# One unit of q less beside the first modulation, two half units of distance in the first GLA head, and fewer modulation steps on TensorE in the branch stage

## The chip, the cores and the metric

The kernel runs on one core of one Trainium2 chip. The metric is the device time of one launch in microseconds. The four compute engines of the core are called by the profile's names: PE (TensorE, matrix products), DVE (VectorE), ACT (ScalarE), POOL (GpSimd). SP issues most DMAs, POOL's queue issues those of the later modulation weights.

## The reference

One layer of a hybrid backbone on 384 tokens of width 2048: 128 context tokens and 256 latent tokens, held side by side as the 384 columns of every product. Cut to what matters here:

```
mod = silu(cond) @ w_ada + b_ada                  # 2048 -> 6 * 2048, for 2 conditions
sh1, sc1, ga1, sh2, sc2, ga2 = split(mod, 6)
h = rmsnorm(x) * (1 + sc1) + sh1
q, k, v, g, lr_f, lr_b, fo = split(h @ w_in)      # q, k: 4 heads x 128, v: 4 x 256
o = gla(q, k, v, decay(lr_f), decay(lr_b))        # chunked scan, both directions, 4 heads
f = real(fft2(fo))                                # per group of 256 channels
gates = sigmoid(h @ w_gate + b_gate)              # 2 * 2048
m = (g_a * (o * silu(g)) @ w_br_gla + g_b * (f @ w_br_four)) @ w_out
x = x + ga1 * rmsnorm(m)
h = rmsnorm(x) * (1 + sc2) + sh2
x = x + ga2 * rmsnorm((silu(h @ w_ffn_gate) * (h @ w_ffn_up)) @ w_ffn_down)
```

All inputs and results are fp32.

## The kernel before, in words

**Products.** Each fp32 operand is split into a high part, a cast to fp32r, and a low part, the difference. A product is three matmuls: high by high, high by low, low by high. For a weight, ACT writes the high part (`whi<-raw`, L300) and DVE the low part (`wlo<-raw`, L287); for an activation the same pair is L378 and L379. A *unit* is 128 output features for all 384 tokens: `proj` runs it as two *half units*, and `gemm` (L326, written `pmm`) issues 24 matmuls of 384 columns for each half unit.

**The first stage** (loop over `kb` from 0 to 15, 128 features of h each). For each `kb`, PE first makes the 256 numbers of shift and scale: `gemv` (L474, `pgm<-slab,spad`) multiplies the condition vector with two slabs of `w_ada1`, 1 MB each, which SP loads into five buffers. Two transposes (L595) and a few DVE instructions turn them into columns, DVE writes the modulated features, ACT and DVE split them. While that runs, PE works on the features of the `kb` before: the product of all of v (`vprod`, L491, `pv`, three groups of six matmuls), and `XU` units of q (`xprod`, L509, three matmuls each for one unit), whose weights `xraw` come in a transfer of their own. Unit 0 uses the PSUM bank `px`, unit 1 from `kb` 3 on the bank `pgm`, which the modulation uses too. DVE adds each finished piece to `xacc` (L504). The order of every engine but SP is that of the code.

**The query, key and gate stage.** The units of q and k that the first stage did not make follow as ordinary units, in the order of `qk_order`, and then 25 units of the gate product. Each half unit but the first unit's calls `side()`, which takes one step of two generators: `gla()`, the small operations of the attention heads, and `ada`, the rest of the modulation. Where `gla()` has a `yield`, the next half unit is put between. In a head, the two directions prepare `qi`, `ki`, `kc`, `ko` on DVE (L851 to L858), one step each. Then PE makes the scores `at` (L875, twelve matmuls for each direction) and `cr`, DVE masks them (L885), some steps later DVE and ACT split `ko` and `att`, and PE makes the state update `dl` and the output `po` (L788).

**The rest of the modulation.** `ada_rest` has six blocks of 1024 columns. A block has 16 `k`-steps, each on a piece of `w_ada` of 512 KB that POOL's queue loads into two buffers (`adaw`). A step runs in one of two ways, by the flag `on_pe`: on DVE as two multiply-adds of 128x1024 (L707, `adacc`), or on PE as four matmuls of 128x256 (L697, `pr<-adaw,spad`). After the steps of a block come an empty call, a call that sums the block over partitions on PE (L718) and one with its transposes (L671).

**The branch stage.** The output gate `g` of the attention and the two branch products are made in `mix_order`: 8 units "o" with a `side()` of their own, 16 pieces "b" of the Fourier branch (`four`, L1239 and L1240), and 16 units "a" of the attention branch, one `gemm` of 24 matmuls each. The first "o" units take modulation steps through `side()` (on PE from its turn 7 on, but for turn 8); the "a" units that the table `TAIL` lists take one each, on PE where it says True. After each "a" unit DVE multiplies by the gate (L1296) and adds (L1297), and one unit later the result is split into `A_hi` and `A_lo` (L379), the right operand of the product with `w_out` that follows. That product's first unit needs `A_lo` of all 16 pieces. The modulation steps that are left run beside `w_out`.

```
if i in TAIL:
    on_pe[0] = TAIL[i]
    next(ada_gen, None)
    on_pe[0] = False
```

Of the kernel before, what the change touches and what calls it, by code (L numbers as in the profile page):

```python
# [25 lines left out]
T = TC + TL  # L26
# [8 lines left out]
FC = 4  # L35
NFC = FT // FC
G = 1024
XU = 2
GF = 25
GD = 256  # L40
TAIL = {1: True, 4: False, 5: True, 8: True, 10: False, 11: True, 13: True, 14: False, 15: False}


C_TRI = 0
# [63 lines left out]
def tile_step(ctx: ExitStack, tc: tile.TileContext, a, o):  # L108
# [49 lines left out]
    srcs = [a["w_v"][k] for k in range(KT)]  # L158
    qk_order = [i for i in (4, 5, *range(XU, 4), 6, 7)]
    for i in qk_order:  # L160
# [250 lines left out]
    with ExitStack() as s:  # L411
# [11 lines left out]
        def load_w(kb):  # L423
            load()
            xraw[kb] = pb.tile([P, XU * P], F32, tag="xraw", name="xraw", bufs=2)
            SP.dma_start(xraw[kb], a["w_x"][kb])
# [39 lines left out]
        pgm = pss.tile([P, 512], F32, tag="side", name="pgm")  # L466
        pgv, pmod = pgm[:, 0:256], pgm[:, 256:512]
        px = pss.tile([P, T], F32, tag="side", name="px")
# [27 lines left out]

        xacc = [pa.tile([P, T], F32, name=f"xacc{u}") for u in range(XU)]
        lracc = pa.tile([P, T], F32, name="lracc")
# [7 lines left out]
        def xprod(u, kb, w, bank=px):  # L506
            def mm():
                for j, (x_, w_) in enumerate(passes(w)):
                    PE.matmul(bank, w_[:, u * P : (u + 1) * P], hT[x_][:, kb, :], start=j == 0, stop=j == 2)  # L509

            return mm, lambda dst=None: flush(xacc[u], kb == 0, dst, bank)
# [38 lines left out]
        prev = None  # L550
        for kb in range(KT):
            if kb and kb + 1 < KT:
                load_slab(kb + 1)
                load_w(kb + 1)
                if kb == 4:
                    load_later()

            wait = kb in (1, 2)
            if kb and not wait:
                gemv(kb)  # L560
            todo = []
            if kb > 4 and kb % 4 == 2:
                todo.append(lrprod(kb - 6))

            both = kb > 2
            if both:
                xs = [xprod(u, kb - 1, prev[1], bank) for u, bank in enumerate((px, pgm[:, 0:T]))]
            elif kb:
                todo += [xprod(u, kb - 1, prev[1]) for u in range(XU)]
            todo += [None] * (4 - len(todo))  # L570
            flushes = [t[1] if t else lambda: None for t in todo]

            def pe_x(n):
                if todo[n]:
                    todo[n][0]()

            if wait:
                vprod(kb - 1, prev[0], (0,))
            pe_x(0)
            hf = scr[:, kb % 8, :]  # L580

            xr = hf if kb else qs[0]
            DVE.tensor_mul(xr, xn(kb), rstd if kb else px)
            flushes[0]()
            if wait:
                gemv(kb)
            if kb:
                ev = pb.tile([P, 256], F32, tag="ev", name="ev")
                ACT.copy(ev, pgv)
            lag = []  # L590
            new = split_w(kb, lag)
            if kb:
                vprod(kb - 1, prev[0], (1 if wait else 0,))
            for m in range(2):
                PE.transpose(pmod[:, m * P : (m + 1) * P], ev[:, m * P : (m + 1) * P], ident)  # L595
            if kb == 0:

                for _ in range(6):
                    PE.matmul(pv[5][:, 0:P], ones, ones, start=True, stop=True)
            pe_x(1)  # L600

            pm = pb.tile([P, 2, 2], F32, tag="pm", name="pm", bufs=2)
            DVE.tensor_reduce(
                pm, pmod.rearrange("p (m q r) -> p m r q", m=2, q=4)[:, :, 0:2, :], axis=mybir.AxisListType.X, op=ALU.add,
            )
            DVE.tensor_scalar(
                mods[:, 1, kb, :], pm[:, 1, :], bsc1[:, 0, kb : kb + 1], norms[:, 0, kb : kb + 1],
                op0=ALU.add, op1=ALU.mult,
            )
            DVE.tensor_scalar_add(mods[:, 0, kb, :], pm[:, 0, :], cols[:, 0, kb : kb + 1])  # L610
            for lo, hi, c in segs:
                DVE.tensor_scalar(
                    hf[:, lo:hi], xr[:, lo:hi], mods[:, 1, kb, c : c + 1], mods[:, 0, kb, c : c + 1],
                    op0=ALU.mult, op1=ALU.add,
                )
                if kb == 0:
                    ACT.activation(
                        hT[0][:, kb, lo:hi], xr[:, lo:hi], AF.Identity,
                        bias=mods[:, 0, kb, c : c + 1], scale=mods[:, 1, kb, c : c + 1],
                    )  # L620
            flushes[1]()
            if kb:
                split_act(hT[0][:, kb, :], hT[1][:, kb, :], hf)
            else:
                ACT.copy(rstd, px)
                DVE.tensor_sub(hT[1][:, kb, :], hf, hT[0][:, kb, :].bitcast(F32))
            if kb:
                if not wait:
                    vprod(kb - 1, prev[0], (1,))
                pe_x(2)  # L630
                flushes[2]()
            if both:
                for mm, _ in xs:
                    mm()
                for _, fl in reversed(xs):
                    fl()
            for sub in lag:
                sub()
            if kb:
                vprod(kb - 1, prev[0], (2,))  # L640
                pe_x(3)
                flushes[3]()
            prev = new
# [109 lines left out]
    with ExitStack() as s:  # L753
# [25 lines left out]
        def gla():  # L779
# [10 lines left out]
            for h in range(NH):  # L790
# [38 lines left out]
                for d in range(2):  # L829


                    bT = pss.tile([P, T], F32, tag="side", name="bT")
                    for t in range(3):
                        for j, l in enumerate((lah, lal)):
                            PE.matmul(
                                bT[:, t * P : (t + 1) * P], l[:, t, d], tri[:, d * P : (d + 1) * P],
                                start=j == 0, stop=j == 1,
                            )
                    sx = pss.tile([P, 2, P], F32, tag="side", name="sx")
                    for j, l in enumerate((lah, lal)):  # L840
                        PE.matmul(
                            sx, tri[:, (2 + d) * P : (3 + d) * P], l[:, 0 : 2 + d : 1 + d, d], start=j == 0, stop=j == 1,
                        )
                    eb = pg.tile([P, T], F32, tag=f"eb{d}", name="eb")
                    ACT.activation(eb, bT, AF.Exp)
                    ki = pg.tile([P, T], F32, tag=f"ki{d}", name="ki")
                    ACT.activation(ki, bT, AF.Exp, scale=-1.0)
                    ko = pg.tile([P, 2, P], F32, tag=f"ko{d}", name="ko")
                    ACT.activation(ko, sx, AF.Exp)
                    qi = pg.tile([P, T], F32, tag=f"qi{d}", name="qi")  # L850
                    DVE.scalar_tensor_tensor(qi, eb, DK**-0.5, qT[:, h, :], op0=ALU.mult, op1=ALU.mult)  # L851
                    DVE.tensor_mul(ki, ki, kT[:, h, :])
                    DVE.tensor_mul(ko, ko, krs[:, 0 : 2 + d : 1 + d, :])

                    last = 0 if d else CH - 1
                    tot = chunks(eb)[:, :, d, last : last + 1]
                    kc = pg.tile([P, 3, CH], F32, tag=f"kc{d}", name="kc")
                    DVE.tensor_mul(kc, chunks(ki)[:, :, d, :], tot.to_broadcast([P, 3, CH]))  # L858
                    dc = pg.tile([P, 1], F32, tag=f"dc{d}", name="dc")
                    c = 5 if d else 2  # L860
                    e0, e1 = c * CH + last, (c + 1 - 2 * d) * CH + last
                    DVE.tensor_mul(dc, eb[:, e0 : e0 + 1], eb[:, e1 : e1 + 1])
                    qin.append(qi)
                    kin.append(ki)
                    kcr.append(kc)
                    kout.append(ko)
                    dec.append((tot, dc))
                    yield

                ats = []  # L870
                for d in range(2):
# [33 lines left out]
                ap = [apt[:, 0], apt[:, 1]]  # L905
                split_act(*ap, att)
                yield
                qpt = [pg.tile([P, 2, 3, P], F32R, tag=t, name="qp") for t in ("lah", "lal")]
                qp = [[q[:, d] for q in qpt] for d in range(2)]
                for d in range(2):  # L910
# [88 lines left out]
    px = fs.enter_context(tc.tile_pool(name="px", bufs=1))  # L999
# [310 lines left out]
    with ExitStack() as s:  # L1310
# [94 lines left out]
        u = pd.tile([P, 2, 3], F32, name="u12", bufs=1)  # L1405
# [355 lines left out]
        bank = {}  # L1761
# [69 lines left out]
        for kind, c, i in steps[:-4]:  # L1831
# [8 lines left out]
            if kind == "D":  # L1840
# [9 lines left out]
                h = hid_last if last_c else hid  # L1850
# [248 lines left out]
```

## Time and profile before

| | us |
|---|---|
| median of three runs | 1943.53 |
| the three runs | 1943.53, 1943.78, 1941.89 |
| the profiled execution | 1942.28 |
| its span | 1940.4 |
| PE busy | 1920.4 (99%) |
| DVE busy | 1647.8 (85%) |
| ACT busy | 916.3 (47%) |

The clock that the throttle granted TensorE was 0.998 of full speed. The time of an execution has 1.9 us that lie outside the span (1942.28 less 1940.4). A row of the timeline gives the start, the duration, the engine, the line, the operation with what it writes and reads, and a count where like instructions follow each other; a bracket at its end says how long the engine was idle before it and what ended that.

### The profile page before, as it was taken

To read this page: it belongs to the slowest core of one execution; us is meant where nothing else is said; L and a number is where in the kernel's file an instruction comes from. 1 tells how busy PE (TensorE), PEld (TensorE's weight loads), DVE (VectorE), ACT (ScalarE), POOL (GpSimd) and SP (SyncE) were. 2 spreads that over 40 slices of the span, in tenths; PEclk is the share of its full clock that TensorE was granted. 3 is DMA by queue.
4 is the path that set the end of the run, shared out by engine and by line. 5 is a ranking of instruction groups with operands and counts; after the bars stand their busy time and mean duration, and the time that the engine had idled before them with its cause. 6 is when DMAs were issued, how large, how long until landed. Compare 5 with 4: busy or idle time off the path is not lost.

```text
span 1940.4 us, 27538 instructions
## 1 busy us (share of the span) xinstructions
PE 1920.4 (99%) x10534; PEld 1690.8 (87%) x10534; DVE 1647.8 (85%) x2172; ACT 916.3 (47%) x1298; POOL 85.8 (4%) x154
## 2 busy tenths in 40 slices
PE   9999999999999999999999999999999999999997
PEld 5779999999999999999988888888888888888886
DVE  5668898889878887978789888999998999888885
ACT  4235455545456554456455444444444444444444
POOL 0001111100000000104000000000000000000001
PEclk9999999999999999999999999999999999999999
DMA  9977766766757885755264636363636272625243
GB/s 390 387 260 248 240 234 227 248 231 194 225 185 246 302 302 181 245 193 198 83 195 131 200 103 194 121 211 98 216 104 213 91 222 93 201 76 185 87 173 110
DMA packets 200615, 380.52 MB, mean 196 GB/s; under 512 B 14196, under 2 KB 126932, under 8 KB 196132
## 3 DMA queue, kind: packets, MB, share of 16 engines
q1 hardware_dynamic: 181252, 320.84, 48.9%
q0 software_dynamic: 13952, 50.39, 8.5%
q10 hardware_dynamic: 5280, 7.55, 1.1%
q8 instruction: 82, 1.34, 0.3%
q14 instruction: 49, 0.40, 0.1%
HBM read 361.94 MB, written 16.78 MB: 195 GB/s over the span
## 4 chain that ended last, share of the span: by engine, by line
PE 93%; DVE 3%; DMA 2%; issue 1%; ACT 1%; SPq 0%; DVEq 0%; ACTq 0%
PE pgu L338 30%; PE pmm L326 30%; PE pdn L338 18%; PE pv L491 3%; PE pgm L474 1%; PE pf L1239 1%; PE pfo L1039 1%; DVE adacc L707 1%; PE pmm L1516 1%; PE ptr L1808 1%; PE pf L1240 1%; PE pfo L1040 1%; DMA xraw<-in_w_x 1%; PE po L788 1%; PE px L509 0%
## 5 line engine op out<-in xcount | busy, mean ns | idle before, releaser
L326 PE MATMUL pmm<-A_hi,whi 128*128 128x384 f32 x1072 | 361.7, 337 | 0.0
L326 PE MATMUL pmm<-A_hi,wlo 128*128 128x384 f32 x1072 | 358.8, 335 | 0.0
L326 PE MATMUL pmm<-A_lo,whi 128*128 128x384 f32 x1072 | 358.6, 335 | 0.0
L1663 ACT CAST whi<-u 128x1024 fp32r<-128x1024 f32 x200 | 210.6, 1053 | 281.5 <-DVE u L1647 86.5
L1663 ACT CAST whi<-raw 128x1024 fp32r<-128x1024 f32 x175 | 184.2, 1052 | 200.8 <-PE pgu L338 63.8
L1674 DVE TENSOR_TENSOR wlo<-u,whi 128x1024 fp32r<-128x1024 f32 x200 | 244.1, 1220 | 32.0 <-ACT whi L1663 18.3
L338 PE MATMUL pgu<-whi,A_hi 128*128 128x512 f32 x640 | 250.0, 391 | 0.0
L338 PE MATMUL pgu<-whi,A_lo 128*128 128x512 f32 x640 | 249.3, 389 | 0.0
L1674 DVE TENSOR_TENSOR wlo<-raw,whi 128x1024 fp32r<-128x1024 f32 x175 | 213.4, 1220 | 34.6 <-ACT whi L1663 25.6
L287 DVE TENSOR_TENSOR wlo<-raw,whi 128x1024 fp32r<-128x1024 f32 x163 | 198.2, 1220 | 24.1 <-ACT whi L300 23.7
L300 ACT CAST whi<-raw 128x1024 fp32r<-128x1024 f32 x149 | 156.0, 1051 | 117.6 <-PE pmm L326 50.0
L326 PEld LDWEIGHTS pmm<-A_hi,whi 128*128 128x128 f32 x1072 | 201.2, 188 | 3.3 <-issue 2.5
L326 PEld LDWEIGHTS pmm<-A_lo,whi 128*128 128x128 f32 x1072 | 201.4, 188 | 0.2
L326 PEld LDWEIGHTS pmm<-A_hi,wlo 128*128 128x128 f32 x1072 | 201.2, 188 | 0.3 <-DVE wlo L287 0.2
L707 DVE SCALAR_TENSOR_TENSOR adacc<-adaw,spad,adacc 128x1024 f32<-128x1024 f32 x160 | 198.1, 1279 | 3.5 <-DMA adaw<-in_w_ada 3.2
L338 PE MATMUL pdn<-whi,hid_hi 128*128 128x512 f32 x480 | 186.9, 389 | 0.0
L338 PE MATMUL pdn<-whi,hid_lo 128*128 128x512 f32 x480 | 186.8, 389 | 0.0
L338 PE MATMUL pgu<-wlo,A_hi 128*128 128x512 f32 x640 | 184.2, 389 | 0.0
L338 PEld LDWEIGHTS pgu<-whi,A_hi 128*128 128x128 f32 x640 | 120.2, 188 | 26.1 <-issue 0.8
L338 PEld LDWEIGHTS pgu<-wlo,A_hi 128*128 128x128 f32 x640 | 120.1, 188 | 25.4
L338 PEld LDWEIGHTS pgu<-whi,A_lo 128*128 128x128 f32 x640 | 120.1, 188 | 25.0
L338 PE MATMUL pgu<-whi,S 128*128 128x512 f32 x480 | 131.1, 395 | 0.0
(405 smaller groups left out, 3042.7 us busy)
## 6 DMA issues: line engine op xcount, KB each, us to landing
adaw<-in_w_ada POOLq DMA_DIRECT2D x96, 512.0 KB, 4.0
raw<-in_w_d SPq DMA_DIRECT2D x88, 512.0 KB, 3.7
slab<-in_w_ada SPq DMA_DIRECT2D x32, 1024.0 KB, 10.2
raw<-in_w_gate SPq DMA_DIRECT2D x64, 512.0 KB, 4.4
raw<-in_w_g SPq DMA_DIRECT2D x48, 512.0 KB, 3.4
raw<-in_w_u SPq DMA_DIRECT2D x48, 512.0 KB, 3.5
raw<-in_w_in SPq DMA_DIRECT2D x44, 512.0 KB, 4.3
u<-in_w_u SPq DMA_DIRECT2D x40, 512.0 KB, 4.6
```

The source lines that it names most:

```text
L287: eng.tensor_sub(lo, raw, hi.bitcast(F32))
L300: ACT.copy(hi, raw)
L326: PE.matmul(dst, w[wi][:, k * n + n0 : k * n + n0 + P], x[xi][:, k0 + k, :], start=first and k == 0 and j == 0, stop=last and k == kts - 1 ...
L338: PE.matmul(dst, stat[x_][m], mov(w[w_], m), start=first and w_ == m == x_ == 0, stop=last and w_ == m == 1,)
L474: PE.matmul(pgv[q : q + 32, :], spad[:, k, :], slab[k // (KT // 2)][:, k % (KT // 2), :], start=k < 4, stop=k >= KT - 4,)
L491: PE.matmul(pv[2 * t + g], hT[x_][:, kb, t * P : (t + 1) * P], w_[:, g * 512 : (g + 1) * 512], start=kb == 0 and j == 0, stop=kb == KT - 1 ...
L707: DVE.scalar_tensor_tensor(acc[:, c, :], w, spad[:, k, c : c + 1], acc[:, c, :], op0=ALU.mult, op1=ALU.add,)
L788: PE.matmul(dst, w[wi], x[xi], start=first and j == 0, stop=last and j == 2)
L1039: PE.matmul(p, w_of[0][:, i, k, g, :], x[:, :, lo:hi], start=kt == 0, stop=False)
L1040: PE.matmul(p[:, 0], w_of[1][:, i, k, g, :], x[:, 0, lo:hi], start=False, stop=kt == KT - 1)
L1663: ACT.copy(hi, src)
L1674: DVE.tensor_sub(lo, src, hi.bitcast(F32))
```

## The change

It does three things. `XU` goes from 2 to 1: the first stage makes q's unit 0 alone, `xraw` is 64 KB and not 128 KB for each `kb`, and unit 1 of q stands as an ordinary unit in `qk_order` after k's units 0 and 1. In head 0 of `gla()` two more `yield`s are put in, one ahead of the scores and one ahead of the state update, so that each of these comes one half unit later after what it reads. In `TAIL` the five places with True are gone or False: 1 and 5 drop out, 8, 11 and 13 run on DVE; the steps of 4, 10, 14 and 15 stay on DVE.

```diff
-XU = 2
+XU = 1
...
-TAIL = {1: True, 4: False, 5: True, 8: True, 10: False, 11: True, 13: True, 14: False, 15: False}
+TAIL = {4: False, 8: False, 10: False, 11: False, 13: False, 14: False, 15: False}
...
             if both:
-                xs = [xprod(u, kb - 1, prev[1], bank) for u, bank in enumerate((px, pgm[:, 0:T]))]
+                xs = [xprod(u, kb - 1, prev[1], bank) for u, bank in enumerate((px, pgm[:, 0:T])[:XU])]
...
                     dec.append((tot, dc))
                     yield
+                if h == 0:
+                    yield
 
                 ats = []
...
                 split_act(*ap, att)
                 yield
+                if h == 0:
+                    yield
                 qpt = [pg.tile([P, 2, 3, P], F32R, tag=t, name="qp") for t in ("lah", "lal")]
```

Counted over the whole program, PE has 48 fewer `xprod` matmuls and 48 more of `pmm`, and 20 fewer of `pr<-adaw`, which are five modulation steps; DVE has ten more L707, which are the same five steps. The number of calls of `ada` up to the start of `w_out` is 87 before and now: the two half units of q's unit 1 take two steps in the query stage, and two places of `TAIL` are gone.

On PE in the first stage, in a `kb` of which both units stood, the difference reads (`px` and `pgm` are the two banks, `pv` is v's):

```order
 L509 MATMUL px<-A_hi,wlo 128x384
 L509 MATMUL px<-A_lo,whi 128x384
-L509 MATMUL pgm<-A_hi,whi 128x384
-L509 MATMUL pgm<-A_hi,wlo 128x384
-L509 MATMUL pgm<-A_lo,whi 128x384
 L491 MATMUL pv<-whi,A_lo 128x512 x6
 L474 MATMUL pgm<-slab,spad 32x256 x16
```

The three matmuls of unit 1 are gone; v's last group and the next `gemv` follow unit 0 directly.

On DVE in head 0, from the second direction's preparation of `ki` to the masking of the scores, before:

```order
L852 TENSOR_TENSOR ki<-ki,qk 128x384
L853 TENSOR_TENSOR ko<-ko,krs 128x256
L858 TENSOR_TENSOR kc<-ki,eb 128x192
L862 TENSOR_TENSOR dc<-eb 128x1
L707 SCALAR_TENSOR_TENSOR adacc<-adaw,spad,adacc 128x1024 x2
L287 TENSOR_TENSOR wlo<-raw,whi 128x1024
L885 COPY_PREDICATED att<-mask,at 64x3x64 x2
```

At the same place now (the first new `yield` shifts the line numbers behind it by two):

```order
L852 TENSOR_TENSOR ki<-ki,qk 128x384
L853 TENSOR_TENSOR ko<-ko,krs 128x256
L858 TENSOR_TENSOR kc<-ki,eb 128x192
L862 TENSOR_TENSOR dc<-eb 128x1
L707 SCALAR_TENSOR_TENSOR adacc<-adaw,spad,adacc 128x1024 x2
L287 TENSOR_TENSOR wlo<-raw,whi 128x1024
L707 SCALAR_TENSOR_TENSOR adacc<-adaw,spad,adacc 128x1024 x2
L287 TENSOR_TENSOR wlo<-raw,whi 128x1024
L887 COPY_PREDICATED att<-mask,at 64x3x64 x2
```

One modulation step and one weight split more stand between the preparation and the masking.

On DVE in the branch stage, at the "a" units 10 and 11, the difference reads (L1296 and L1297 are now L1300 and L1301):

```order
 L243 TENSOR_TENSOR ws<-raw 128x512
 L244 TENSOR_TENSOR ws<-raw 128x512
-L1296 TENSOR_TENSOR gate<-gate,pmm 128x384
-L1297 TENSOR_TENSOR yb<-yb,gate 128x384
+L1300 TENSOR_TENSOR gate<-gate,pmm 128x384
+L1301 TENSOR_TENSOR yb<-yb,gate 128x384
 L379 TENSOR_TENSOR A_lo<-yb,A_hi 128x384
+L707 SCALAR_TENSOR_TENSOR adacc<-adaw,spad,adacc 128x1024 x2
 L287 TENSOR_TENSOR wlo<-ws,whi 128x1024
 L287 TENSOR_TENSOR wlo<-raw,whi 128x1024
```

The modulation step of unit 11 now stands on DVE, ahead of two weight splits.

## The prediction

> **What bounds the kernel now.** I read the page first: the busy times, and the chain of work that ended last.
>
> ```profile
> span 1940.4 us, 27538 instructions
> PE 1920.4 (99%) x10534; PEld 1690.8 (87%) x10534; DVE 1647.8 (85%) x2172; ACT 916.3 (47%) x1298; POOL 85.8 (4%) x154
> PE 93%; DVE 3%; DMA 2%; issue 1%; ACT 1%; SPq 0%; DVEq 0%; ACTq 0%
> ```
>
> PE is idle for 20 us of the span. So a matmul taken off PE is worth its time, where nothing else makes PE wait at that place; and a matmul put on costs its time. All three parts of the change have to be priced as PE time first, and then each place has to be looked at for what comes late instead. I looked at them in the order of the program: the chain of waits in the first stage, its transfers, the timeline of PE and DVE in the first attention head, and the same two in the branch stage.
>
> **The change part by part: the first stage.** The chain there, and one row of the weight loads' timeline:
>
> ```profile
> 40.53 1.39 PE pv L491 x6
> 41.92 0.54 PE px L509 x3
> 42.45 0.53 PE pgm L509 x3
> 42.98 1.39 PE pv L491 x6
> 44.37 1.86 PE pgm L474 x32
> 60.13 0.61 PEld L474 LDWEIGHTS pgm<-slab,spad 128*32 128x32 f32 x16 [0.25 <-DMA slab<-in_w_ada]
> 128.80 1.86 PE pgm L474 x32
> ```
>
> Unit 1's three matmuls are the 0.53 us on `pgm`. There are 16 such groups, one for each `kb`, so PE loses 16 x 0.53 = 8.5 us of work. That is the upper bound of this part's gain. Not all of it can count: at 60.13 the second half of `kb` 6's `gemv` started the moment its slab had landed (PE's loader had been idle 0.25 us for it), so up to there the stage goes no faster than its transfers.
>
> ```profile
> slab<-in_w_ada SPq DMA_DIRECT2D x10, 1024.0 KB, 11.1
> raw<-in_w_v SPq DMA_DIRECT2D x5, 512.0 KB, 8.1
> xraw<-in_w_x SPq DMA_DIRECT2D x5, 128.0 KB, 8.0
> 20.00:50.00 30.00, 29.51 (x229) 20.32 (x228) 18.55 (x44) 9.81 (x19) 0.00 (x0) 1.00 1.02 414
> 60.00:85.00 25.00, 25.00 (x209) 17.70 (x202) 15.62 (x37) 7.04 (x14) 0.00 (x0) 1.00 1.02 414
> 85.00:125.00 40.00, 40.00 (x314) 28.80 (x313) 24.57 (x57) 11.80 (x22) 0.00 (x0) 1.00 0.97 359
> ```
>
> The last number of a windows row is GB/s. A `kb` moves two slabs, one `raw` and one `xraw`: 2.75 MB before, 2.69 MB now (half of `xraw`, 65.5 KB, is gone). Up to `kb` 6 that is about six halves, 0.39 MB, at 414 GB/s 0.95 us sooner. From there on the `gemv` of `kb` 7 to 15 have nine groups fewer ahead of them, and two more groups lie behind the last `gemv`: 11 x 0.53 = 5.8 us, if the slabs keep up. Together the gain is 6.8 us.
>
> Do the slabs keep up? The last two were issued right after PE had read a slab for the last time:
>
> ```profile
> L474 PE MATMUL pgm<-slab,spad x2: 379/379/379, 114.6 to 114.6; 128*32 128x256 f32 x2
> L419 SPq DMA_DIRECT2D slab<-in_w_ada x2: 382/382/382, 114.9 to 115.4; - x2
> DMA to landing us min/median/max: 10.6/10.6/10.6
> ```
>
> The last landed at 115.4 + 10.6 = 126.0, and the second half of the last `gemv` needed it at about 128.80 + 0.93 = 129.7. So there was 3.7 us of slack at the end of the stage against nearly none at `kb` 6: the transfers had gained on PE. Now PE gains 9 x 0.53 = 4.8 us on that stretch, and the transfers' issue, which waits for PE to free a buffer, comes earlier with it, and 9 x 65.5 KB less are to be moved (0.59 MB, 1.4 us at 414 GB/s). A slack of 3.7 + 1.4 = 5.1 covers 4.8, so I take 6.8. The bounds are 8.5, as if nothing waited, and 4.3, from the first rival.
>
> **Unit 1 of q as a unit of its own.** It costs 48 matmuls of `pmm`.
>
> ```profile
> 673.21 4.21 PE pmm L326 x24
> 677.42 0.57 PE pr L697 x8
> 677.99 8.55 PE pmm L326 x48
> 720.90 29.33 PE pmm L326 x168
> ```
>
> In a long run one takes 29.33/168 = 0.1746 us, so 48 take 8.4 us. Its weights add two transfers of 512 KB and two splits, in a stage that has one of each for every half unit already. A half unit gives DVE 4.2 us for one split (1.21) and one modulation step (2.47, both below), so I charge nothing more. This eats the first stage's gain and more: −6.8 + 8.4 = +1.6.
>
> **The first attention head.** PE's timeline at head 0, with DVE's rows beside it, the pair of score groups of the next head (from the chain), and what the state update waits for:
>
> ```profile
> 191.34 0.57 PE L875 MATMUL at<-qi,ki 128*64 128x64 f32 x12
> 193.46 0.57 PE L875 MATMUL at<-qi,ki 128*64 128x64 f32 x12 [1.55 <-DVE ki L852]
> 260.96 0.85 PE at L875 x24
> 191.16 1.21 DVE L287 TENSOR_TENSOR wlo<-raw,whi 128x1024 fp32r<-128x1024 f32 x1
> 192.30 0.54 DVE L851 SCALAR_TENSOR_TENSOR qi<-eb,qk 128x384 f32<-128x384 f32 x1
> 192.77 0.54 DVE L852 TENSOR_TENSOR ki<-ki,qk 128x384 f32<-128x384 f32 x1
> 211.38 0.72 PE dl L788 x6
> 210.49 0.75 DVE L379 TENSOR_TENSOR part<-ko,part 128x256 fp32r<-128x256 f32 x2
> ```
>
> The second direction's scores start 193.46 − 191.34 = 2.12 us after the first's, where a group takes 0.85/2 = 0.43: PE waits 1.7 us for `ki`, which DVE ends at 193.31. The first new `yield` puts a half unit of 4.2 us ahead of the scores, and DVE makes `ki` as early as before (the order of its rows up to there is the same). So the scores are wanted at about 195.5, `ki` is there 2.2 us sooner, and the 1.7 us go. That also takes away the delay behind which `dl` found its operands: it started at 211.38, and DVE's `part` of `ko` had ended at 211.24, 0.14 before. Without the second `yield`, PE coming 1.7 us earlier there would wait for most of it again; with it there are again 4.2 us between. Gain 1.7, its bounds 0 and 1.7.
>
> **Five modulation steps from PE to DVE.** On PE a step costs its own 0.57 us and a little around it: the rows from 673.21 to 686.54 take 4.21 + 0.57 + 8.55 = 13.33 us for 72 matmuls, which at 0.1746 would take 12.57. So 0.76 each, and 3.8 us for five.
>
> On DVE each costs two L707. Three of the five stand in the "a" units that stay (8, 11, 13); DVE's timeline there:
>
> ```profile
> 706.88 2.47 DVE L707 SCALAR_TENSOR_TENSOR adacc<-adaw,spad,adacc 128x1024 f32<-128x1024 f32 x2
> 709.27 0.69 DVE L243 TENSOR_TENSOR ws<-raw 128x512 f32<-128x512 f32 x1
> 698.12 0.56 DVE L1296 TENSOR_TENSOR gate<-gate,pmm 128x384 f32<-128x384 f32 x1 [1.00 <-PE pmm L326]
> 702.28 0.55 DVE L1296 TENSOR_TENSOR gate<-gate,pmm 128x384 f32<-128x384 f32 x1 [1.41 <-PE pmm L326]
> 717.99 0.55 DVE L1296 TENSOR_TENSOR gate<-gate,pmm 128x384 f32<-128x384 f32 x1 [0.97 <-PE pmm L326]
> 725.30 0.55 DVE L1296 TENSOR_TENSOR gate<-gate,pmm 128x384 f32<-128x384 f32 x1 [1.50 <-PE pmm L326]
> 736.47 1.23 DVE L379 TENSOR_TENSOR A_lo<-yb,A_hi 128x384 fp32r<-128x384 f32 x2
> ```
>
> A step takes DVE 709.27 − 706.88 = 2.39 us, so three add 7.2. In the brackets DVE stood idle for PE for 1.00 + 1.41 + 0.97 + 1.50 = 4.9 us, which the added work fills. The steps of units 1 and 5 are gone from PE before this stretch, so DVE, which waits for PE there, enters it 2 x 0.76 = 1.5 us earlier. Left over is 7.2 − 4.9 − 1.5 = 0.8: the last `A_lo`, done at 736.47 + 1.23 = 737.70, is done at 738.5. PE wants it in the first unit of `w_out`, at the 119th of the 168 matmuls from 720.90 (72 of units 13 to 15, then 15 pieces of three, then the one by the low part): 720.90 + 118 x 0.1746 = 741.5, a slack of 3.8. But PE is now 3.8 us earlier, and wants it at 737.7. It waits 0.8 us. The bounds are 0 and 1.5, if the 1.5 us are not passed on. The other two added DVE steps take the places of `side()` turns in the "o" units where PE had them; a "o" half unit gives DVE the same 4.2 us, and I charge nothing.
>
> **The sum.** −6.8 + 8.4 − 1.7 − 3.8 + 0.8 = −3.1 us. The profiled execution took 1942.28 (1.9 us around its span), and with the three runs the mean of four is 1942.9. I take 1942.6 as the base, between the two: 1942.6 − 3.1 = 1939.5. By the profiled execution alone it would be 1939.2, by the median of 1943.53 it would be 1940.4.
>
> **The rivals.** *The transfers hold the first stage.* The third windows row moved only 359 GB/s. If that is all that the queue gives from `kb` 6 on, a `kb` takes 2.69 MB/359 GB/s = 7.48 us, and from 60.13 less 0.95 the slab of `kb` 15 comes at 59.2 + 9 x 7.48 = 126.5 in place of the need at 129.7: 3.2 us gained there and 1.1 behind it, 4.3 in all. The sum is then −0.6, the time 1942.0. Against it: in that stretch PE took (128.80 − 60.13)/9 = 7.63 us for a `kb`, and 2.75 MB in 7.63 us is 361 GB/s, which is what PE asked for; and the rows before it have 414. [...]
>
> *The first stage gains all of it.* If the wait at 60.13 comes from a slab that fewer bytes and an earlier free buffer bring earlier, all 16 groups count and the branch stage loses nothing: −8.5 + 8.4 − 1.7 − 3.8 = −5.6, so 1937.0. For it: the wait at 60.13 is only 0.25 us. Against it: slabs were already landing at the full 414 GB/s there.
>
> *VectorE becomes the bound of the branch stage.* The idle in the brackets is time in which DVE waited for PE; if something that DVE itself feeds (a weight's low part) comes late for PE at units 8 to 13, PE stops, and the brackets fill no longer. Then the 7.2 us of the three steps come through whole instead of 0.8: the sum is −3.1 + 6.4 = +3.3, the time 1945.9, slower than before. It decides as soon as DVE's delay passes the slack that the weight splits have, which by the last `A_lo` is 3.8 us before and nothing now. Against it: DVE stood idle for PE at four units' gates in the rows above.
>
> *The wait of the first head stays.* If the scores or `dl` wait as long at their new place, 1.7 us are lost again: 1941.2. Against it stands 2.2 us of slack.
>
> **How the numbers follow.** The forecast has 0.55, the transfers 0.15, the full gain 0.14, VectorE 0.10, the wait that stays 0.06. About 0.2% (3.9 us) is what a measurement of this kernel can tell from no change, so faster begins below 1939.6 and slower above 1947.4. The forecast lies on the lower of these bounds, its own range being 1937.5 (the lower base of 1942.28 and all 8.5 us of the first stage) to 1941.1 (the median as the base and a wait of 1.5 for `A_lo`); I count 0.28 of it as faster and 0.27 as the same. The full gain adds 0.14 to faster: 0.42. The transfers, the wait that stays and half of VectorE's case are within: 0.27 + 0.15 + 0.06 + 0.05 = 0.53. The other half of VectorE's case, with a second wait behind the first, is slower: 0.05. The range goes from 1936.0, the full gain less half the 1.9 us by which the three runs differ, to 1944.5, which takes in the transfers and the part of VectorE's case in which half of the 6.4 us comes through, and leaves out the rest.
>
> **What would show it right or wrong.** In the profile after: the chain of the first stage should have no `pgm L509`, and the last `gemv` should start near 128.80 − 0.95 − 4.8 = 123.1; a bracket with `slab` at `kb` 10 to 15 would be the first rival. The second `at` group should follow the first by 0.4 us, and `dl` should have no bracket. The rows `pr L697` among the "a" units should be gone, with PE's "a" units following each other by 4.2 us and one wait under 1.5 us for `A_lo` some 50 matmuls into `w_out`. A bracket with `wlo` or `A_lo` of several microseconds would prove the VectorE case. A time above 1944.5 would mean that a wait came in which I did not see; one below 1936.0 that PE's idle, not its work, was what the change took away.

## The result, and the profile after

| | before | after |
|---|---|---|
| median | 1942.61 (22 runs) | 1939.58 (22 runs) |
| lowest to highest | 1941.39 to 1944.13 | 1938.76 to 1940.83 |
| the profiled execution, its span | 1942.28, 1940.4 | 1939.26, 1937.5 |

The ratio is 0.9985, with a 95% interval of 0.9979 to 0.999. The forecast was 1939.5, 3.1 us less than its base of 1942.6; measured are 3.0 us less. The page of the changed kernel, the same three lines as of before:

```profile
span 1937.5 us, 27470 instructions
PE 1916.2 (99%) x10494; PEld 1689.0 (87%) x10494; DVE 1650.8 (85%) x2168; ACT 915.3 (47%) x1301; POOL 85.8 (4%) x154
PE 92%; DMA 3%; DVE 3%; ACT 1%; issue 0%; SPq 0%; DVEq 0%; ACTq 0%
```

PE has 4.2 us less work (the 40 instructions fewer are the 20 matmuls of the five modulation steps, each of which the profile shows as two), and the span is 2.9 us shorter. PE's idle time grew by 1.3 us (1937.5 − 1916.2 against 1940.4 − 1920.4). To see where, take the two programs at places that both have, first of the kernel before and then of the changed one: the first matmuls of the first k unit (a row with two times gives the start of the first and of the last matmul that it counts), the second head's scores (before, they stand in the prediction, at 260.96), the first modulation step on PE in the o units, and the block's sum beside `w_out`:

```profile
L326 PE MATMUL pmm<-A_hi,whi x2: 338/342/346, 142.3 to 142.8; 128*128 128x384 f32 x2
...
L697 PE MATMUL pr<-adaw,spad x8: 379/391/403, 590.6 to 590.8; 128*32 128x256 f32 x8
...
750.23 1.00 PE pr L718 x16
```

```profile
L326 PE MATMUL pmm<-A_hi,whi x14: 333/334/346, 135.8 to 142.6; 128*128 128x384 f32 x14
...
260.88 0.85 PE at L877 x24
...
L697 PE MATMUL pr<-adaw,spad x8: 379/391/403, 590.5 to 590.7; 128*32 128x256 f32 x8
...
747.57 1.00 PE pr L718 x16
```

The first stage ends 6.5 us sooner (142.3 to 135.8). At the next head's scores the lead is 0.1, and 0.1 at 590: the unit of q, less the head's wait, has taken it. The lead comes back between 590 and 750: 2.7 us (750.23 to 747.57). So nearly all of the net gain is made in the branch stage, as the sum had it (−0.1 up to there, −3.0 in it).

The details, first of the first stage: the loader's row at `kb` 6, the chain at the end of the stage, then two windows whose last number is GB/s.

```profile
59.46 0.59 PEld L474 LDWEIGHTS pgm<-slab,spad 128*32 128x32 f32 x16 [1.39 <-DMA slab<-in_w_ada]
121.48 0.54 PE px L509 x3
122.02 1.40 PE pv L491 x6
123.41 1.86 PE pgm L474 x32
60.00:85.00 25.00, 25.00 (x199) 17.57 (x192) 13.75 (x36) 7.71 (x15) 0.00 (x0) 1.00 1.02 413
85.00:120.00 35.00, 35.00 (x288) 24.25 (x287) 20.67 (x49) 10.15 (x20) 0.00 (x0) 1.00 0.98 380
```

`pgm L509` is gone. The wait at `kb` 6 is longer, 1.39 us in place of 0.25, and the second half of that `gemv` starts 0.67 sooner (60.13 to 59.46), not 0.95. The last `gemv` starts at 123.41, against 123.1 expected and 128.80 before. The last windows row has 380 GB/s where it had 359: the queue gave more when PE asked for more, and no `gemv` after `kb` 6 waits for its slab. That closes the first rival, whose rate of 359 was PE's demand.

Then the head: DVE's `ki`, PE's chain.

```profile
186.64 0.55 DVE L852 TENSOR_TENSOR ki<-ki,qk 128x384 f32<-128x384 f32 x1
136.01 8.35 PE pmm L326 x48
189.11 0.85 PE at L877 x24
211.32 0.72 PE dl L788 x6
```

Both score groups run in one piece, 0.85 us, and `ki` (ended at 187.19) was there 2.3 us before its group at 189.5; 2.2 were expected. A unit of 48 matmuls takes 8.35.

Then the branch stage: two `pf` matmuls of the chain as they run without a wait, the places where PE waits, the last two `A_lo` (pieces 14 and 15, in one row), and the chain from the first wait for them to the block's sum:

```profile
599.98 0.20 PE pf L1243
600.18 0.09 PE pf L1244
612.24 0.34 PE L1243 MATMUL pf<-edT,whi 128*128 128x388 f32 x1
612.86 0.36 PE L1244 MATMUL pf<-edT,wlo 128*128 128x194 f32 x1 [0.28 <-DVE wlo L287]
613.05 0.36 PE L1243 MATMUL pf<-edT,whi 128*128 128x388 f32 x1
...
737.33 1.22 DVE L379 TENSOR_TENSOR A_lo<-yb,A_hi 128x384 fp32r<-128x384 f32 x2
737.30 0.34 PE L326 MATMUL pmm<-A_hi,whi 128*128 128x384 f32 x1
737.94 0.44 PE L326 MATMUL pmm<-A_lo,whi 128*128 128x384 f32 x1 [0.30 <-DVE A_lo L379]
738.22 0.34 PE L326 MATMUL pmm<-A_hi,wlo 128*128 128x384 f32 x1
...
738.61 0.44 PE L326 MATMUL pmm<-A_lo,whi 128*128 128x384 f32 x1
738.89 0.34 PE L326 MATMUL pmm<-A_hi,wlo 128*128 128x384 f32 x1
...
737.94 9.63 PE pmm L326 x53
```

The block's sum comes behind 96 matmuls of `w_out` (in the prediction's row of 168, 72 belong to the units), and 53 of them run from 737.94 on. So the matmul that waited there is the 44th of `w_out`, in the prediction's count the 116th, which reads the `A_lo` of piece 14; the 119th, with that of piece 15, follows at 738.61, when the row of `A_lo` has ended (738.55; the prediction had 738.5). From 737.30 to 738.89 PE started five matmuls in 1.59 us in place of 0.87, so the two together cost 0.7; 0.8 was expected, at the 119th alone. The stall on a weight's low part at 612.86 was not: 0.81 us from 612.24 to 613.05, where such a pair takes 0.20 + 0.09, so 0.5.

### The profile page after: what moved, and what is told of

It reads as the page before. It is cut to its first block, busy times and chain, and to the rows that moved or that the text cites. A ratio compares the mean times of both kernels' runs of the same rounds, so it can differ in the third digit from the quotient of the medians.

```text
span 1937.5 us, 27470 instructions
## 1 busy us (share of the span) xinstructions
PE 1916.2 (99%) x10494; PEld 1689.0 (87%) x10494; DVE 1650.8 (85%) x2168; ACT 915.3 (47%) x1301; POOL 85.8 (4%) x154
## 4 chain that ended last, share of the span: by engine, by line
PE 92%; DMA 3%; DVE 3%; ACT 1%; issue 0%; SPq 0%; DVEq 0%; ACTq 0%
PE pgu L338 31%; PE pmm L326 31%; PE pdn L338 18%; PE pv L491 3%; DMA slab<-in_w_ada 2%; PE pfo L1043 1%; PE pf L1243 1%; PE pgm L474 1%; PE pmm L1520 1%; PE ptr L1812 1%; PE pfo L1044 1%; PE pf L1244 1%; PE po L788 1%; DVE wlo L287 0%; DMA raw<-in_w_br_gla 0%
## 5 line engine op out<-in xcount | busy, mean ns | idle before, releaser
L326 PE MATMUL pmm<-A_hi,whi 128*128 128x384 f32 x1088 | 366.9, 337 | 0.0
L326 PE MATMUL pmm<-A_lo,whi 128*128 128x384 f32 x1088 | 364.1, 335 | 0.3 <-DVE A_lo L379 0.3
L326 PE MATMUL pmm<-A_hi,wlo 128*128 128x384 f32 x1088 | 364.2, 335 | 0.0
L707 DVE SCALAR_TENSOR_TENSOR adacc<-adaw,spad,adacc 128x1024 f32<-128x1024 f32 x170 | 210.4, 1279 | 3.3 <-DMA adaw<-in_w_ada 3.1
```

The source lines that it names most:

```text
L326: PE.matmul(dst, w[wi][:, k * n + n0 : k * n + n0 + P], x[xi][:, k0 + k, :], start=first and k == 0 and j == 0, stop=last and k == kts - 1 ...
L707: DVE.scalar_tensor_tensor(acc[:, c, :], w, spad[:, k, c : c + 1], acc[:, c, :], op0=ALU.mult, op1=ALU.add,)
```

## The experiments

Each kernel was timed beside the kernel before on the same chip; the median of before was 1942.7, 1942.8 and 1942.9 in the three batches.

**The first part alone.** The change without the yields and with the old `TAIL`:

```diff
-XU = 2
+XU = 1
...
+                xs = [xprod(u, kb - 1, prev[1], bank) for u, bank in enumerate((px, pgm[:, 0:T])[:XU])]
```

> Kernel before with the first part alone: one unit of q in the first stage, unit 1 as an ordinary unit; no new yields, the old table TAIL. Theory A, the three parts add up on PE at three separate places: the first stage ends 6.5 us sooner (by the profiles of before and after), the unit costs 8.4, the wait of 1.7 us in the first head stays: 1.9 us slower than before, 1944.5 at a base of 1942.6. Theory B, the parts need each other: the two half units more give the heads' generator room for its last steps (62 steps for 62 calls, where before 2 steps were left over behind the gates), which brings up to 1 us back: 1943.5. Theory C, the first stage gives nothing because transfers hold it: 8.4 slower, 1951.

Measured: 1947.31, 1.0022 of before (1.0013 to 1.0031), 4.7 us slower. None of the three theories has that. PE's and DVE's timeline in head 0, one matmul behind it, and two windows (the third number from the end is the granted clock):

```profile
184.50 0.57 PE L875 MATMUL at<-qi,ki 128*64 128x64 f32 x12
188.24 0.57 PE L875 MATMUL at<-qi,ki 128*64 128x64 f32 x12 [3.17 <-DVE ki L852]
187.54 0.55 DVE L852 TENSOR_TENSOR ki<-ki,qk 128x384 f32<-128x384 f32 x1
191.20 0.52 PE L326 MATMUL pmm<-A_hi,wlo 128*128 128x384 f32 x1
184.00:188.50 4.50, 1.33 (x25) 0.97 (x25) 4.50 (x7) 2.38 (x3) 0.80 (x2) 1.00 0.48 169
189.40:192.60 3.20, 3.20 (x11) 3.17 (x11) 3.19 (x5) 0.00 (x0) 0.53 (x1) 0.53 0.44 179
```

The wait for `ki` did not stay, it grew from 1.55 to 3.17 us. PE came 6.8 us sooner to the scores (191.34 to 184.50), DVE ended `ki` only 5.2 sooner (193.31 to 188.09). And behind the wait the granted clock was 0.53 for 3.2 us: about 1.5 us more. In this profile the first k unit starts at 135.45, so the sum −6.9 + 8.35 + 1.6 + 1.5 = 4.6 gives most of the 5.0 us by which the two spans differ (1945.4 and 1940.4).

**The second part alone**, the two yields on the kernel before (these two lines at both places):

```diff
+                if h == 0:
+                    yield
```

> Kernel before with the second part alone: the two new yields in head 0; two units of q in the first stage, the old TAIL. Theory A: the 1.7 us wait of the second score group goes, everything else stays: 1940.9 at a base of 1942.6. Theory B, the parts need each other: 64 steps of the heads' generator now meet 60 calls, four steps are left over behind the gates in place of two, and what PE loses there eats 1 to 2 us: 1942 to 1943.

Measured: 1941.98, 0.9998 of before (0.9989 to 1.0007): 0.7 us by the medians, not told apart from nothing. Theory B is nearer, and its place shows in the profile, DVE first and then PE, shortly behind the last gate unit:

```profile
440.21 0.23 DVE L946 RECIPROCAL rs<-rs 128x12 f32<-128x12 f32 x1 [2.39 <-ACT rs L945]
457.77 0.44 PE L326 MATMUL pmm<-A_hi,wlo 128*128 128x384 f32 x1 [1.26 <-DVE wlo L287]
```

The last steps of the heads are left over, DVE waits 2.39 us for their sums, and PE waits 1.26 us for a weight's low part behind them. PE came to the stretch behind the gates 2.0 us sooner than in the kernel before (the first `pfo` matmul starts at 453.71 and 455.74) and DVE to that weight 0.6 (456.49 and 457.12), so most of what the yields had gained is lost there. The unit of q, with its two half units, is what makes room for the yields' two steps.

**The third part alone**, the new `TAIL` on the kernel before:

> Kernel before with the third part alone: the new TAIL; two units of q in the first stage, no new yields. The calls of the modulation up to w_out are 85 and not 87, two more are made beside w_out. Theory A: five steps less on PE at 0.76 us are 3.8 us, less a wait of 0.7 us for the last A_lo: 3 us faster, 1939.6. Which steps are on DVE differs from the changed kernel, since the blocks lie two calls later: a stall of about 0.5 us more or less among the o units is open. Theory B, the modulation that is left over comes back beside w_out (two steps of 2.4 us on DVE that nothing covers): 1942 to 1944.

Measured: 1941.04, 0.9991 of before (0.9982 to 1.0), 1.6 us faster where theory A has 3. Theory B's place is there in the profiled execution (with 1943.26 one of the kernel's longer ones), late in `w_out`, where the last block of the modulation is summed:

```profile
841.77 0.64 PE L718 MATMUL pr<-adacc,selr 128*32 128x256 f32 x8 [1.06 <-DVE adacc L707]
842.87 0.64 PE L718 MATMUL pr<-adacc,selr 128*32 128x256 f32 x8 [0.46 <-DVE adacc L707]
844.00 0.69 PE L671 MATMUL ptm<-ident,adev 128*128 128x128 f32 x2 [0.49 <-ACT adev L667]
```

With 85 calls up to `w_out` in place of 87 the last block ends behind its last steps, and PE waits for each piece. In this execution the `pmm` matmuls behind the last of these waits also start 0.32 us apart, from 844.81 to 847.05, where those from 847.32 on start 0.17 apart; whether the median one, 2.2 us shorter, has that too is not shown.

Alone, the three parts come to +4.7 − 0.7 − 1.6 = +2.4; together to −3.0. Each of the three has an interval of about ±1.8 us, and the gap is 5.4. They are no three terms.

**The first two parts together**, that is, the changed kernel with the old `TAIL`:

> The changed kernel with the old table TAIL: one unit of q in the first stage and both new yields, so it differs from the run with the first part alone only in the yields. That run lost 3.4 us at the scores of head 0 and some 1.5 us more to a lower granted clock right behind. Theory A, the yields cover all of that: 5 us less than that run's 1947.3, so 1942.3, and the rest of the way to the changed kernel's 1939.6 is the table's 2.7 us. Theory B, the yields are worth the 1.7 us of the sum, as in the prediction: 1945.6, and the table would then be worth 6 us.

Measured: 1943.03, 0.9999 of before (0.999 to 1.0008). Theory A's 1942.3 is 0.7 off, theory B's 1945.6 is 2.6 off. On the way from before the first part adds 4.7, the yields then take 4.3, and the table takes 3.4. The wait at 612.86 is in this kernel too:

```profile
613.70 0.36 PE L1244 MATMUL pf<-edT,wlo 128*128 128x194 f32 x1 [0.28 <-DVE wlo L287]
```

It is in the run with the first part alone as well (0.28 us at 617.43). So it belongs not to the table but to the two calls of the modulation that the unit of q brings, which shift the blocks against the o units: in the changed kernel two modulation steps on DVE fall among these units, at 586.30 and 601.64, where the kernel before has none.

**Without the second yield**, the one ahead of the state update:

> The changed kernel without the second new yield, the one ahead of the state update; the first stays. Theory A, the prediction's: the update's first product finds its operand (part, from ko) 0.9 to 1.6 us late and waits for it: 1940.5 to 1941.2 against 1939.6. Theory B, the first yield alone is enough, since DVE's and ACT's work on ko has a half unit of its own either way: 1939.6, or a little less, as one step less of the heads' generator is left over.

Measured: 1942.73, 3.1 us more than with it. Theory A has the place; the price is twice what it says:

```profile
208.94 0.75 PE L788 MATMUL dl<-vr,part 128*128 128x256 f32 x4 [1.95 <-DVE part L379]
210.30:213.50 3.20, 3.20 (x12) 3.20 (x11) 3.20 (x4) 0.00 (x0) 0.53 (x1) 0.50 0.72 279
```

A wait of 1.95 us, and again 3.2 us at half the clock behind it. The profiled execution is the longest of its eleven (1944.48), so whether the median's 3.1 us holds the half clock too is not shown.

**The small loads one `kb` later**, for the wait at `kb` 6:

```diff
-                if kb == 4:
+                if kb == 5:
                     load_later()
...
-            if kb > 4 and kb % 4 == 2:
-                todo.append(lrprod(kb - 6))
+            if kb > 4 and kb % 4 == 3:
+                todo.append(lrprod(kb - 7))
```

> The changed kernel with the small loads (309 KB in all: low-rank weights, gate bias and others) issued one kb later, behind the slabs of kb 6, and the low-rank products of kb 6, 10, 14 moved to kb 7, 11, 15 so that their weights are there. In the changed kernel PE's loader stood idle 1.39 us at kb 6 for the slab, and nowhere after. Theory A, that wait is the price of the small loads that stand ahead of the slab: at 414 GB/s they take 0.75 us, so the stage ends 0.7 us sooner, up to 1.4: 1938.2 to 1938.9, against 1939.6. Theory B, the slabs are held by the whole queue and the wait only moves to kb 7: no difference to the changed kernel, 1939.6.

Measured: 1939.13, 0.9983 of before (0.9974 to 0.9991), 0.4 us less than the changed kernel, which the intervals do not tell apart.

```profile
65.34 0.63 PEld L474 LDWEIGHTS pgm<-slab,spad 128*32 128x32 f32 x16 [0.23 <-DMA slab<-in_w_ada]
```

The wait of 1.39 at `kb` 6 is gone and one of 0.23 is left at `kb` 7, so theory A is right on the wait. The stage's gain of about 1 us does not reach the end whole. The profiled execution, 1.0 us longer than this kernel's median, has two waits that the changed kernel's profile has not: 0.61 us at 222.26 for `adev` and 0.64 us at 521.83 for a weight's low part. The profile with unit 14 out of `TAIL` (below) has the same two, 0.87 and 0.44 us, without the later loads; so they need not come from this change, and what became of the gain in the other executions stays open.

**Two more steps on DVE in the a units**, `TAIL` with 9 and 12 too:

> The changed kernel with two more modulation steps on DVE in the branch stage, at units 9 and 12 (89 calls up to w_out in place of 87, two less beside w_out). Theory A, DVE has no slack left at the last A_lo, where PE already waits 0.5 to 0.7 us: 2 x 2.39 us come through nearly whole, less what little idle DVE has left, so 3.5 to 4.8 us slower than the changed kernel, 1943.1 to 1944.4, unless the two steps less beside w_out give some back. Theory B, what is late for PE is not DVE's sum but single weights, and the steps fill idle: 1939.6 to 1941.

Measured: 1941.96, 2.4 us more than the changed kernel, between the two theories. PE waits at two places:

```profile
716.78 0.36 PE L1244 MATMUL pf<-edT,wlo 128*128 128x194 f32 x1 [1.33 <-DVE wlo L287]
740.33 0.45 PE L326 MATMUL pmm<-A_lo,whi 128*128 128x384 f32 x1 [0.96 <-DVE A_lo L379]
```

The first wait gives DVE time to catch up, so the second is 0.96 and not 4: a weight's low part is late before the sum of DVE's work is.

**One step less in the a units**, unit 14 out of `TAIL`:

> The changed kernel with one modulation step less in the branch stage (unit 14 out of TAIL; 86 calls up to w_out, one more beside it). Theory A, the wait for the last A_lo goes, 0.5 to 0.7 us, and nothing else happens: 1938.9 to 1939.1. Theory B, the last block of the modulation gets late: the run with the table alone had 85 calls, and its profile shows PE waiting some 4 us in w_out for the last block's sum; one call less than now would bring 1 to 4 us of that: 1940 to 1943.

Measured: 1940.01, 0.9987 of before (0.9978 to 0.9996), 0.4 us more than the changed kernel, which the intervals do not tell apart. The wait for `A_lo` is gone from the profile (1941.45, one of the longer executions), and in its place stands

```profile
843.49 0.44 PE L671 MATMUL ptm<-ident,adev 128*128 128x128 f32 x2 [1.02 <-ACT adev L667]
```

which is theory B's place, at its small end: by this profile 87 calls up to `w_out` are just enough.

**Steps on DVE in the o units**, on top of the later loads: turns 9 and 13, then all five.

```diff
-                on_pe[0] = turn[0] > 6 and turn[0] != 8
+                on_pe[0] = turn[0] in (7, 11, 15)
```

> The changed kernel with the small loads one kb later (as in the run before), and the modulation steps of turns 9 and 13 in the o units on DVE too. Theory A, a step on PE costs 0.76 us, and DVE stands idle 0.58 + 0.39 + 1.17 = 2.1 us in an o unit of the changed kernel's profile, so a step of 2.39 fits but for 0.3 us, with a stall of 0.4 us in the Fourier piece behind it as the profile has after turn 8: 2 x (0.76 - 0.4) = 0.7 us faster than the 1939.1 of the run with the later loads, 1938.4. Theory B, DVE has nothing left, the steps delay the last A_lo and PE waits there for all of it: 1939.1 + 2 x 2.39 - 1.5 = 1942.4.

> As the run with turns 9 and 13 on DVE, but all the modulation steps of the o units on DVE (turns 7, 9, 11, 13, 15): no step of the modulation is left on PE. Theory A: 5 x 0.76 = 3.8 us less on PE, five stalls of 0.4, and a DVE that enters the a units 5 x 0.3 = 1.5 us later, which comes through at the last A_lo: 1939.1 - 3.8 + 2.0 + 1.5 = 1938.8, about where it was. Theory B, DVE is the bound as soon as two units with a step follow each other: the 12 us of the five steps less 5 x 2.1 us of idle less nothing else, and waits for weights in each o unit of over 1 us: 1941 or more.

Measured: 1945.36 and 1950.49, 6.2 and 11.4 us more than the kernel that they start from. Of the 11.4 us 1.7 are a stretch of 3.41 us at half the clock behind idle time of PE (the last section). The mean granted clock of the profiled execution is 0.998 in the first and 0.996 over 1949.2 us in the second, so the lower clock costs the second some 4 us, an estimate from clocks that are rounded to 0.001; the first has 1.00 in every window from 576 to 760 us. The first one's waits at turn 9:

```profile
613.07 0.45 PE L1243 MATMUL pf<-edT,whi 128*128 128x388 f32 x1 [1.99 <-ACT whi L294]
614.33 0.36 PE L1244 MATMUL pf<-edT,wlo 128*128 128x194 f32 x1 [0.81 <-DVE wlo L287]
```

One step of 2.39 us on DVE makes PE wait 2.8 us, although DVE has 2.1 us of idle in such a unit: DVE folds the Fourier weight there, ACT casts what it folded, DVE makes the low part, and PE waits at the end of these three. The idle lies behind that series, not ahead of it.

## Why the prediction was right, point by point

- **The sum** held: −3.1 against −3.0. It held because each term was priced at the place where the whole change puts it: the scores' slack of 2.2 us was worked out with the yield in, and was 2.3 (0.7 to 2.3 in the eight traces with this yield behind one unit of q, so the yield covers it in all). That it came within 0.1 us is luck in part: the first stage gave 0.3 and the branch stage 0.4 less than expected, the head 0.3 more, and some 0.2 came behind the branch stage.
- **The first stage**: −6.8 in the sum, −6.5 in the profile. The wait at `kb` 6 did not shrink with the bytes; it grew by 1.1 us, as PE came sooner and the slab 0.67. The run with the later loads shows that the small loads ahead of the slab were most of the reason.
- **The unit of q**: +8.4, measured 8.35.
- **The head**: −1.7 is near the difference of the two kernels (−2.0, by the lead of 0.1 at the next head's scores: 6.5 − 8.4 + 2.0), and wrong as the worth of the yields. The wait that it removes is not the same in every execution: in the profile with the third part alone, whose program up to there is that of the kernel before, it is 0.62 us and not 1.55. With the first stage shorter the same wait was 3.2 us, and 1.5 more by the clock; the yields are worth 4.3 us in the change and 0.7 by themselves. The prediction treated DVE's `ki` as moving with PE; DVE gained 1.6 us less. The fourth rival (the wait stays, 1941.2) had its place right and its price much too low: without the second yield alone it was 1942.7.
- **Five steps off PE**: −3.8 + 0.8 = −3.0; the profile has −2.7 + 0.1 = −2.6 between 590 and 750, which −3.8, 0.7 for `A_lo` and 0.5 at 612 make up. The 0.5 the prediction put at nothing: it saw two DVE steps come among the o units, but in the place of steps on PE and without a stall, while PE kept its five there. The table's worth as measured by the timed runs was 3.4.
- **VectorE as the bound** did not come. The runs show where it would: two more steps in the o units cost 6.2 us, two more in the a units 2.4. The prediction named the right mechanism, a weight's low part that comes late, and put it at units 8 to 13; the sharper place is the o units.

## What to carry to other kernels

When one part of a change makes an engine arrive sooner, every wait that this engine has on another one behind that point grows by as much as the other does not follow (here from 1.55 to 3.17 us); price the wait at its new size, and judge the parts together, since a part that looks worthless alone (here the yields, 0.7 us) may be what lets another pay. A queue of equal steps has to come out even: a unit added in one stage made the room that two added steps needed, and the same two steps without it were left over at the end. Idle time of an engine can be filled only if it lies ahead of the work that others wait for (here 2.1 us of it did not, and a step of 2.39 us cost a wait of 2.8).

## What the runs showed of the hardware

A wait of PE had a second price in some of these runs. Behind the waits of 3.17 and of 1.95 us the granted clock was 0.53 and 0.50 in the windows of 3.2 us above, about 1.5 us lost each time; behind the wait of 1.55 us in the kernel before it was 1.00.

The length of one wait did not decide it: behind the wait of 1.99 us in the run with two steps on DVE in the o units the clock was 1.00 as well. Three pairs of stretches of 3.41 us follow, with waits in the first of each pair: all five steps, the kernel before, two steps; then a longer window of the run with two steps. The first number after the comma is PE's busy time, the third from the end the clock.

```profile
648.38:651.79 3.41, 1.70 (x10) 1.44 (x11) 3.02 (x4) 3.39 (x5) 0.00 (x0) 1.00 0.46 159
651.80:655.21 3.41, 3.41 (x14) 3.41 (x14) 2.88 (x9) 1.00 (x3) 0.00 (x0) 0.50 0.66 202
...
190.10:193.51 3.41, 1.86 (x22) 1.51 (x21) 3.41 (x5) 1.04 (x1) 0.80 (x2) 1.00 0.41 149
193.51:196.92 3.41, 3.41 (x38) 3.34 (x39) 3.41 (x6) 0.00 (x0) 0.24 (x1) 1.00 0.70 253
...
612.56:615.97 3.41, 2.09 (x12) 1.82 (x13) 3.00 (x5) 3.38 (x6) 0.00 (x0) 1.00 0.53 166
615.97:619.38 3.41, 3.41 (x22) 3.41 (x22) 2.53 (x7) 1.02 (x2) 0.00 (x0) 1.00 0.74 227
...
610.00:625.00 15.00, 12.20 (x80) 10.96 (x79) 12.72 (x25) 9.29 (x14) 1.05 (x2) 1.00 0.68 217
```

With all five steps PE was idle for 1.71 us in the first stretch, and the clock was 0.50 for the 3.41 us behind it, which is 1.7 us lost. In the other two pairs PE was idle for 1.55 and 1.32 us, and the clock behind was 1.00. The wait of 1.99 us ended at 613.07 and began before 612.56, so its row holds only a part of it; with the 0.81 us that follow, PE was idle for 2.80 us from 610 to 625 (15.00 less 12.20), and the clock there was 1.00 too. So the idle time by itself does not tell the cases apart, and these rows do not show what does.
